# Eight offsets for the weight tiles and three pass sequences, in place of one of each

## The chip, the cores and the metric

The kernel runs on one core of a Trainium2 chip. The metric is the device time of one execution in microseconds (us). A profiled execution gives, beside its time, a trace of every instruction on every engine: TensorE (PE, with its weight loads as PEld), VectorE (DVE), ScalarE (ACT), GpSimd (POOL) and SyncE (SP).

## What is computed

Two decoder layers on 256 tokens of width 2048, in float32. The first mixes by retention, the second by sliding-window attention; after each comes a gated feed-forward with a short convolution:

```
for i in range(DEPTH):                       # DEPTH = 2
    hn = rmsnorm(h, norm_mix_g[i])
    h = h + (retention(hn, ...) if i == 0 else sliding_window_attention(hn, ...))
    hn = rmsnorm(h, norm_ffn_g[i])
    u = hn @ w_up                            # 2048 x 11008
    c = conv_b + sum(pad(u)[:, j:j+S] * conv_w[j] for j in range(3))
    a, b = split(c, 2)
    h = h + (silu(a) * b) @ w_down           # 5504 x 2048
return rmsnorm(h, final_norm_g)
```

Retention projects to q and k (8 heads of 256), v and a gate (8 heads of 512) and back; attention projects to 32 query heads and 4 key and value heads of 64 and back. Almost all of the work is in these projections.

## The kernel before

Every weight is read once from HBM, in transfers of up to 1 MB: a `Unit` is one transfer of up to 2048 columns per partition (several chunks of 128 weight rows side by side), and the units form one list over the whole kernel. Each number is split in two parts of reduced precision, hi and lo: ScalarE makes hi of a raw tile (L161), VectorE makes lo as the rest (L162), in pieces of 1024 columns, some way ahead of TensorE, into four buffers of each. Activations are split likewise into tiles xT, yT and zT, a chunk being [128, 2, 256]: 256 columns of hi and 256 of lo.

A product is then three parts: hi by hi, hi by lo, lo by hi. There are two forms. `products` (L256 to L258) holds a slice of the activations stationary and moves 512 (for the values of attention 256) weight columns past it, three passes into one PSUM bank. It makes v and the gate of retention, the values of attention and all projections back. `products_tr` gives a transposed result and is used for q, k and the up-projection. It holds 128 weight columns stationary and moves the activations: a long pass (L267) holds hi weights and moves 512 columns, activations hi and lo at once; a short pass (L269) holds lo weights and moves 256. A chunk of a group has two 128-column halves with a bank each. In the letters that the change uses, H and h are the long passes of the first and second half, L and l the short ones, and the sequence is HhLl.

hi and lo tiles are 2048 + 64 columns wide, so that a unit's data can be set off from the tile's start. The offset `at` is 48 columns (192 bytes) in each unit that has a transposed group, and 0 in all others. In the built program all buffers of hi, lo, xT, yT, zT, v, vs, sch and pT begin on a multiple of 256 bytes within a partition, and the slices that a pass takes are whole multiples of 256 bytes further on. So the distance between the stationary slice and the moving chunk, modulo 256 bytes, is 4 x `at` in `products_tr`, and 0 in `products`, but for the values of attention, which share a unit with the keys and so have 192 bytes on the moving side (that is 64, counted from the moving to the stationary slice). Transposes (L276) hold a slice of h, pr or y stationary and move the identity; the tile h lies 32 bytes past a multiple of 64 bytes, pr and y lie on one.

The order of work is set by Python as the program is written out: `run_main` walks over the units, emits a unit's passes, and calls `split_ahead` and a list of small tasks (evictions, norms, scores) between chunks. The scheduler leaves this order as it is.

Of the kernel before, what the change touches and what calls it, by code (L numbers as in the profile page):

```python
# [16 lines left out]
P = 128  # L17
D = 2048
S = 256
# [26 lines left out]
RAW = 2  # L46
SPLIT = 1024

ASIDE = 48
F_CUTS = [0, 14, 28, NF]  # L50
START = (1, 1, 2, 2, 2)

# [57 lines left out]
class Kernel:  # L110
# [37 lines left out]
    def splits(self, i):  # L148

        u = self.units[i]  # L150
        nc = self.nc
        w = u.n * u.cols
        at = ASIDE if any(g.tr for g in u.groups) else 0
        u.hi, u.lo = (
            self.wp.tile([P, 2048 + 64], F32R, tag=tag, name=tag, bufs=AHEAD + 1)[:, at : at + w]
            for tag in ("hi", "lo")
        )
        for c in range(0, w, SPLIT):
            e = min(c + SPLIT, w)
            raw, hi, lo = (x[:, c:e] for x in (u.raw, u.hi, u.lo))  # L160
            nc.scalar.copy(out=hi, in_=raw)  # L161
            nc.vector.tensor_tensor(out=lo, in0=raw, in1=hi.bitcast(F32), op=ALU.subtract)  # L162
            yield e / w
# [29 lines left out]
    def run_main(self):  # L193
        for i, u in enumerate(self.units):
            self.load_to(i + AHEAD + RAW)
            self.split_ahead(i)
            for g in u.groups:
                if g.ps is None:
                    if g.begin:
                        g.begin()  # L200
                    g.ps = self.banks(g)
            if u.groups[0].by_token:
                break
            for j, g in enumerate(u.groups):
                c0 = sum(x.cols for x in u.groups[:j])
                for kk, ch in enumerate(u.chunks):
                    sl = slice(kk * u.cols + c0, kk * u.cols + c0 + g.cols)
                    if g.tr:
                        self.products_tr(g, u.hi[:, sl], u.lo[:, sl], u.act[ch])
                    else:  # L210
                        for t in range(2):
                            out = g.ps[t] if g.apart else g.ps[:, t]
                            self.products(g, out, t, u.hi[:, sl], u.lo[:, sl], u.act[ch])
                    g.seen += 1
                    self.step += g.cols / 512
                    if g.seen == g.total:
                        g.done(g)
                    share = (self.step - u.at) / u.steps
                    self.split_ahead(i, share - 1e-6)
                    self.run_tasks()  # L220
        self.run_by_token(self.units[i:])
        while self.tasks:
            self.step += 1
            self.run_tasks()
# [32 lines left out]
        nc.tensor.matmul(out, lhsT=ah, rhs=lo, start=False, stop=False)  # L257
        nc.tensor.matmul(out, lhsT=al, rhs=hi, start=False, stop=last)  # L258

    def products_tr(self, g, hi, lo, act):  # L260

        nc = self.nc
        first, last = g.seen == 0, g.seen == g.total - 1
        both = act.rearrange("p x s -> p (x s)")
        tiles = [(g.ps[:, i], slice(i * P, (i + 1) * P)) for i in range(2)]
        for out, sl in tiles:
            nc.tensor.matmul(out, lhsT=hi[:, sl], rhs=both, start=first, stop=False)  # L267
        for out, sl in tiles:
            nc.tensor.matmul(  # L269
                out[:, :S], lhsT=lo[:, sl], rhs=act[:, 0], start=False, stop=last  # L270
            )


    def transposes(self, ps, ins):
# [683 lines left out]
```

## Time and profile before

| | |
|---|---|
| median of 2 runs | 2431.38 us (2431.19 to 2431.57) |
| the profiled execution's own time | 2431.45 us |
| its span, first to last instruction | 2429.3 us |
| mean granted TensorE clock | 0.999 |
| PE busy | 2413.0 us (99%), 12676 matmuls |
| DVE busy | 1554.9 us (64%) |
| ACT busy | 1224.6 us (50%) |
| moved by DMA | 460.27 MB, mean 189 GB/s |

The span is what the trace covers, 2 us less than the time of the execution. Matmuls are pipelined: a record's end is modelled, records overlap, and so the time that a pass takes on the engine is read from start to start.

### The profile page before, as it was taken

The numbers are of one execution on the slowest core, as the hardware profiler recorded it, in microseconds if no ns is written. First come the engines' busy times: TensorE is split into PE (matmuls) and PEld (weight loads), VectorE is DVE, ScalarE is ACT, GpSimd is POOL, SyncE is SP. The second block draws the span as 40 slices with busy tenths as digits, with TensorE's granted clock in tenths as the row PEclk, the third lists the DMA queues.
The fourth block names the chain that finished last, engine by engine and source line by source line (L and its number), as shares of the span: only waits on it lengthen the run. The fifth ranks groups of instructions, "written<-read, shape, count | busy, mean of one in ns | idle before, by whom it ended". The sixth has DMA issues, their size and how long they took to land.

```text
span 2429.3 us, 31370 instructions
## 1 busy us (share of the span) xinstructions
PE 2413.0 (99%) x12676; PEld 2060.6 (85%) x12676; DVE 1554.9 (64%) x2104; ACT 1224.6 (50%) x1782; POOL 29.2 (1%) x37
## 2 busy tenths in 40 slices
PE   8999999999999999999999999999999999999998
PEld 7888888888888888888888888888888888888887
DVE  6555555554556775677577756876777477657774
ACT  6444344344445553555355545765555355535553
POOL 3000000000000000000000000000000000000000
PEclk9999999999999999999999999999999999999999
DMA  8655555555554555555555555445454555554553
GB/s 287 213 187 180 192 181 186 185 188 182 182 191 168 199 185 194 192 192 183 197 192 195 194 182 195 182 156 193 174 194 174 207 191 191 190 207 175 195 200 126
DMA packets 68977, 460.27 MB, mean 189 GB/s; under 512 B 8032, under 2 KB 9184, under 8 KB 16736
## 3 DMA queue, kind: packets, MB, share of 16 engines
q1 hardware_dynamic: 68544, 457.23, 52.7%
q8 instruction: 99, 1.62, 0.3%
q10 hardware_dynamic: 288, 1.05, 0.1%
q14 instruction: 46, 0.38, 0.0%
HBM read 456.15 MB, written 2.10 MB: 189 GB/s over the span
## 4 chain that ended last, share of the span: by engine, by line
PE 97%; DMA 1%; issue 1%; POOL 0%; DVE 0%; ACT 0%; SPq 0%; POOLq 0%; DVEq 0%; ACTq 0%
PE mm L267 33%; PE mm L269 17%; PE mm L256 13%; PE mm L258 12%; PE mm L257 12%; PE po L256 2%; PE po L258 2%; PE po L257 2%; PE po L393 1%; PE ms L276 1%; PE ms L679 1%; PE ms L503 0%; POOL acc L309 0%; DMA h<-in_xT 0%; DVE lo L162 0%
## 5 line engine op out<-in xcount | busy, mean ns | idle before, releaser
L162 DVE TENSOR_TENSOR lo<-raw,hi 128x1024 fp32r<-128x1024 f32 (+1 forms) x849 | 1018.4, 1219 | 612.3 <-ACT hi L161 611.9
L161 ACT CAST hi<-raw 128x1024 fp32r<-128x1024 f32 (+1 forms) x849 | 857.8, 1042 | 522.5 <-PE mm L258 332.3
L267 PE MATMUL mm<-xT,hi 128*128 128x512 f32 x3552 | 1107.9, 393 | 6.2 <-DVE xT L323 6.2
L269 PEld LDWEIGHTS mm<-xT,lo 128*128 128x128 f32 x3552 | 667.3, 188 | 150.3 <-DVE lo L162 3.1
L269 PE MATMUL mm<-xT,lo 128*128 128x256 f32 x3552 | 702.2, 279 | 1.1 <-DVE lo L162 1.0
L267 PEld LDWEIGHTS mm<-xT,hi 128*128 128x128 f32 x3552 | 540.5, 188 | 11.7 <-ACT hi L161 6.2
L256 PE MATMUL mm<-hi,zT 128*128 128x512 f32 x688 | 268.3, 390 | 0.0
L258 PE MATMUL mm<-hi,zT 128*128 128x512 f32 x688 | 267.7, 389 | 0.0
L257 PE MATMUL mm<-lo,zT 128*128 128x512 f32 x688 | 267.7, 389 | 0.0
L601 DVE SCALAR_TENSOR_TENSOR cv<-u,cw,cv 128x255 f32<-128x255 f32 x344 | 158.3, 481 | 6.1
L256 PE MATMUL mm<-hi,yT 128*128 128x512 f32 x384 | 153.3, 399 | 0.0
L258 PEld LDWEIGHTS mm<-hi,zT 128*128 128x128 f32 x688 | 129.1, 188 | 27.0
L257 PEld LDWEIGHTS mm<-lo,zT 128*128 128x128 f32 x688 | 129.2, 188 | 26.5
L256 PEld LDWEIGHTS mm<-hi,zT 128*128 128x128 f32 x688 | 129.1, 188 | 26.4
L258 PE MATMUL mm<-hi,yT 128*128 128x512 f32 x384 | 149.8, 390 | 0.0
L257 PE MATMUL mm<-lo,yT 128*128 128x512 f32 x384 | 149.7, 390 | 0.0
L378 ACT COPY u<-mm 128x512 f32<-128x512 f32 x86 | 50.4, 586 | 183.7 <-PE mm L269 183.7
L379 DVE TENSOR_TENSOR u<-mm,u 128x512 f32<-128x512 f32 x86 | 59.5, 692 | 93.2 <-ACT u L378 93.2
L594 ACT ACTIVATE cv<-u,cw 128x256 f32<-128x256 f32 x172 | 94.2, 595 | 48.7 <-DVE u L388 48.7
L611 ACT CAST zT<-cv 128x256 fp32r<-128x256 f32 x86 | 34.9, 406 | 156.2 <-DVE cv L609 156.2
L256 PE MATMUL mm<-hi,xT 128*128 128x512 f32 (+1 forms) x288 | 109.1, 379 | 0.0
L258 PE MATMUL mm<-hi,xT 128*128 128x512 f32 (+1 forms) x288 | 108.6, 377 | 0.0
(118 smaller groups left out, 1784.1 us busy)
## 6 DMA issues: line engine op xcount, KB each, us to landing
raw<-in_up SPq DMA_DIRECT2D x172, 1024.0 KB, 4.7
raw<-in_ret_in SPq DMA_DIRECT2D x94, 1024.0 KB, 4.8
raw<-in_dn SPq DMA_DIRECT2D x72, 1024.0 KB, 4.8
raw<-in_ret_out SPq DMA_DIRECT2D x32, 1024.0 KB, 4.7
raw<-in_qkv SPq DMA_DIRECT2D x20, 1024.0 KB, 4.7
raw<-in_att_out SPq DMA_DIRECT2D x14, 1024.0 KB, 4.7
raw<-in_dn SPq DMA_DIRECT2D x16, 512.0 KB, 3.2
raw<-in_dn SPq DMA_DIRECT2D x8, 768.0 KB, 4.3
```

Of the source, the lines that this page charges most:

```text
L161: nc.scalar.copy(out=hi, in_=raw)
L162: nc.vector.tensor_tensor(out=lo, in0=raw, in1=hi.bitcast(F32), op=ALU.subtract)
L256: nc.tensor.matmul(out, lhsT=ah, rhs=hi, start=first, stop=False)
L257: nc.tensor.matmul(out, lhsT=ah, rhs=lo, start=False, stop=False)
L258: nc.tensor.matmul(out, lhsT=al, rhs=hi, start=False, stop=last)
L267: nc.tensor.matmul(out, lhsT=hi[:, sl], rhs=both, start=first, stop=False)
L269: nc.tensor.matmul(out[:, :S], lhsT=lo[:, sl], rhs=act[:, 0], start=False, stop=last)
L378: nc.scalar.copy(out=x, in_=g.ps[:, :, S:])
L379: nc.vector.tensor_tensor(out=x, in0=g.ps[:, :, :S], in1=x, op=ALU.add)
L594: nc.scalar.activation(out=c[:, half], in_=u[:, half], func=AF.Identity, scale=w[:, 2:3], bias=w[:, 3:4])
L601: nc.vector.scalar_tensor_tensor(out=c[:, half, d:], in0=u[:, half, : S - d], scalar=w[:, 2 - d : 3 - d], in1=c[:, half, d:], op0=ALU.mult ...
L611: nc.scalar.copy(out=z[:, 0], in_=s)
```

## The change

The one offset becomes a list of eight, taken in turn by a unit's number in the list of all units. A unit's number divided by eight, modulo three, gives its `order`: 0 keeps HhLl; 1 is HLhl; 2 is HhLl with every other chunk turned round to LlHh (not the last chunk of a group). Units without a transposed group keep offset 0 and use no order. Of 1776 transposed chunks, 672 become HLhl, 224 become LlHh and 880 stay HhLl. Of 3552 long passes (and as many short ones) 448 each have the offsets 0, 12, 16, 40 and 44, 432 have 48, 428 have 52 and 452 have 56.

```
-ASIDE = 48
+ASIDE = (56, 52, 48, 44, 40, 16, 12, 0)
...
-        at = ASIDE if any(g.tr for g in u.groups) else 0
+        at = ASIDE[i % len(ASIDE)] if any(g.tr for g in u.groups) else 0
+        u.order = i // len(ASIDE) % 3
...
-                        self.products_tr(g, u.hi[:, sl], u.lo[:, sl], u.act[ch])
+                        self.products_tr(g, u.hi[:, sl], u.lo[:, sl], u.act[ch], u.order)
...
-        tiles = [(g.ps[:, i], slice(i * P, (i + 1) * P)) for i in range(2)]
-        for out, sl in tiles:
-            nc.tensor.matmul(out, lhsT=hi[:, sl], rhs=both, start=first, stop=False)
-        for out, sl in tiles:
-            nc.tensor.matmul(
-                out[:, :S], lhsT=lo[:, sl], rhs=act[:, 0], start=False, stop=last
-            )
+        seq = {0: "HhLl", 1: "HLhl", 2: "HhLl"}[order]
+        if order == 2 and g.seen % 2 and not last:
+            seq = "LlHh"
+        for x in seq:
+            i = int(x.islower())
+            out, sl = g.ps[:, i], slice(i * P, (i + 1) * P)
+            if x in "Hh":
+                nc.tensor.matmul(out, lhsT=hi[:, sl], rhs=both, start=first, stop=False)
+            else:
+                nc.tensor.matmul(
+                    out[:, :S], lhsT=lo[:, sl], rhs=act[:, 0], start=False, stop=last
+                )
```

On TensorE, in the first two chunks of the q and k weights of the second retention head (a unit of offset 0 and order 1), the program of before has these rows. The names are out<-moving,stationary with buffer numbers; "x2" is two in a row. L267 is the long line, L269 the short one.

```order
L267 MATMUL mm_693<-xT_118,hi_594 128x512 x2
L269 MATMUL mm_693<-xT_118,lo_595 128x256 x2
L267 MATMUL mm_693<-xT_120,hi_594 128x512 x2
L269 MATMUL mm_693<-xT_120,lo_595 128x256 x2
L393 MATMUL po_708<-v_539,sch_569 128x512 x3
```

In the program after, where the long line is L275, the short one L277 and the attached products L401, the same place reads:

```order
L275 MATMUL mm_693<-xT_118,hi_594 128x512
L277 MATMUL mm_693<-xT_118,lo_595 128x256
L275 MATMUL mm_693<-xT_118,hi_594 128x512
L277 MATMUL mm_693<-xT_118,lo_595 128x256
L275 MATMUL mm_693<-xT_120,hi_594 128x512
L277 MATMUL mm_693<-xT_120,lo_595 128x256
L275 MATMUL mm_693<-xT_120,hi_594 128x512
L277 MATMUL mm_693<-xT_120,lo_595 128x256
L401 MATMUL po_708<-v_539,sch_569 128x512 x3
```

Long and short passes take turns; the work of other lines stands where it stood. One unit later (offset 56, order 2) TensorE had, before:

```order
L267 MATMUL mm_693<-xT_142,hi_632 128x512 x2
L269 MATMUL mm_693<-xT_142,lo_633 128x256 x2
L267 MATMUL mm_693<-xT_144,hi_632 128x512 x2
L269 MATMUL mm_693<-xT_144,lo_633 128x256 x2
L267 MATMUL mm_693<-xT_152,hi_632 128x512 x2
```

and after:

```order
L275 MATMUL mm_693<-xT_142,hi_632 128x512 x2
L277 MATMUL mm_693<-xT_142,lo_633 128x256 x2
L277 MATMUL mm_693<-xT_144,lo_633 128x256 x2
L275 MATMUL mm_693<-xT_144,hi_632 128x512 x2
L275 MATMUL mm_693<-xT_152,hi_632 128x512 x2
```

The four short passes of two chunks now stand together, and so do the four long ones around the next border. The order of instructions on ScalarE, SyncE and GpSimd is the same in both programs; VectorE's is too, with a few waits for TensorE left out.

## Rows read from the trace of the kernel before

**Rows 1.** The page: busy time of each engine, and the granted clock in 40 slices.
```profile
PE 2413.0 (99%) x12676; PEld 2060.6 (85%) x12676; DVE 1554.9 (64%) x2104; ACT 1224.6 (50%) x1782; POOL 29.2 (1%) x37
...
PEclk9999999999999999999999999999999999999999
```

**Rows 2.** The page: the chain that ended last, by line.
```profile
PE mm L267 33%; PE mm L269 17%; PE mm L256 13%; PE mm L258 12%; PE mm L257 12%; PE po L256 2%; PE po L258 2%; PE po L257 2%; PE po L393 1%; PE ms L276 1%; PE ms L679 1%; PE ms L503 0%; POOL acc L309 0%; DMA h<-in_xT 0%; DVE lo L162 0%
```

**Rows 3.** Waits of PE: who for whom, us in total, times, longest.
```profile
PE mm L267 <- DVE xT L323: 6.2, 1, 6.2
PE mm L269 <- DVE lo L162: 1.0, 3, 0.5
```

**Rows 4.** Timeline of PE at 790 us: start us, us, line, count.
```profile
790.28 0.62 PE L267 MATMUL mm<-xT,hi 128*128 128x512 f32 x2
790.74 0.39 PE L269 MATMUL mm<-xT,lo 128*128 128x256 f32 x2
790.97 0.62 PE L267 MATMUL mm<-xT,hi 128*128 128x512 f32 x2
```

**Rows 5.** PE groups by line and form: count, busy us, mean ns, idle before.
```profile
L267 PE MATMUL mm<-xT,hi 128*128 128x512 f32 x3552 | 1107.9, 393 | 6.2 <-DVE xT L323 6.2
L269 PE MATMUL mm<-xT,lo 128*128 128x256 f32 x3552 | 702.2, 279 | 1.1 <-DVE lo L162 1.0
L256 PE MATMUL mm<-hi,zT 128*128 128x512 f32 x688 | 268.3, 390 | 0.0
...
L257 PE MATMUL mm<-lo,zT 128*128 128x512 f32 x688 | 267.7, 389 | 0.0
...
L393 PE MATMUL po<-pT,vs 128*64 128x256 f32 x96 | 16.3, 278 | 0.0
...
L257 PE MATMUL mm<-lo,xT 128*128 128x256 f32 x32 | 9.0, 281 | 0.0
```

**Rows 6.** The same groups in five windows of some 50 ns from 1000.49 us.
```profile
L267 PE MATMUL mm<-xT,hi 128*128 128x512 f32 x1 | 0.4, 388 | 0.0
...
L267 PE MATMUL mm<-xT,hi 128*128 128x512 f32 x1 | 0.4, 392 | 0.0
L269 PE MATMUL mm<-xT,lo 128*128 128x256 f32 x1 | 0.3, 283 | 0.0
...
L269 PE MATMUL mm<-xT,lo 128*128 128x256 f32 x1 | 0.3, 280 | 0.0
...
L267 PE MATMUL mm<-xT,hi 128*128 128x512 f32 x1 | 0.4, 394 | 0.0
L269 PE MATMUL mm<-xT,lo 128*128 128x256 f32 x1 | 0.3, 276 | 0.0
```

**Rows 7.** Instructions of L267, L269 and L257: duration ns min/median/max.
```profile
L267 PE MATMUL mm<-xT,hi x3552: 387/392/794, 6.2 to 2338.6; 128*128 128x512 f32 x198
...
L269 PE MATMUL mm<-xT,lo x3552: 276/280/415, 7.3 to 2339.0; 128*128 128x256 f32 x198
...
L257 PE MATMUL mm<-lo,zT x688: 387/389/398, 905.7 to 2420.3; 128*128 128x512 f32 x172
```

**Rows 8.** Instructions of L276, the transposes: duration ns min/median/max.
```profile
L276 PE MATMUL ms<-ident,h x96: 270/272/273, 696.4 to 1716.9; 128*128 128x128 f32 x96
L276 PE MATMUL ms<-ident,pr x96: 272/272/273, 1514.0 to 1661.6; 128*128 128x128 f32 x96
```

**Rows 9.** Groups: the weight loads of L269, and the splits on DVE and ACT.
```profile
L269 PEld LDWEIGHTS mm<-xT,lo 128*128 128x128 f32 x3552 | 667.3, 188 | 150.3 <-DVE lo L162 3.1
...
L162 DVE TENSOR_TENSOR lo<-raw,hi 128x1024 fp32r<-128x1024 f32 (+1 forms) x849 | 1018.4, 1219 | 612.3 <-ACT hi L161 611.9
L161 ACT CAST hi<-raw 128x1024 fp32r<-128x1024 f32 (+1 forms) x849 | 857.8, 1042 | 522.5 <-PE mm L258 332.3
```

More of the change, by code (lines that the diff above doesn't have):

```diff
@@ L258, in products, with products_tr @@
         nc.tensor.matmul(out, lhsT=al, rhs=hi, start=False, stop=last)
-    def products_tr(self, g, hi, lo, act):
+    def products_tr(self, g, hi, lo, act, order):
         nc = self.nc
```

## Prediction

> **What bounds the kernel now.** The first view is the share of busy time, and it leaves one candidate: TensorE is busy 2413.0 of 2429.3 us, and its granted clock is at full speed in all 40 slices [rows 1], so there is no slow clock to win back. The chain of waits says the same from the other end: nearly all of it is TensorE's own matmuls, half of them the two lines that the change touches [rows 2]. TensorE's waits are the third view: one of 6.2 us for the first activations and three of 1.0 us in all for a lo tile, both where the kernel starts [rows 3]. So nothing that VectorE, ScalarE or a transfer does can be won on this path. What counts is the time from one matmul's start to the next one's start, times their number.
>
> That time has to be read with care, because a matmul's record is longer than its share of the engine. In the steady stretch at 790 us one chunk (two long, two short passes) repeats every 0.69 us [rows 4], while the four records of such a chunk, at the means, last 2 x 393 + 2 x 279 = 1344 ns [rows 5]. The record is longer than the step by (1344 - 690) / 4, about 163 ns, in every pass. So a pass whose record is 4 ns longer costs 4 ns, and differences of records are prices.
>
> **What the change does, part by part.** It moves nothing between engines. The same 3552 long and 3552 short passes run on the same tiles. Two things differ for them: how far the stationary slice lies from the moving chunk (modulo 256 bytes; the moving chunks all lie on multiples of 256 bytes), and which pass follows which.
>
> *Sequence.* The records of two chunks that follow each other, pass by pass [rows 6], are H 388, h 392, L 283, l 280 and then H 392, h 394, L 276, l 276 (the second H and l repeat figures of rows that stand there). Averaged over the two chunks, a long pass before a load of hi costs 390 and before a load of lo 393; a short pass before a load of lo costs 279.5, before a load of hi 278. I take the price of a pass to hang on its own length and on what is loaded under it. In HLhl both long passes stand before lo and both short ones before hi: 2 x 393 + 2 x 278 = 1342 against 390 + 393 + 279.5 + 278 = 1340.5, so +1.5 ns for each of 672 chunks, +1.0 us. In a pair HhLl LlHh, three of four long passes stand before hi and three of four short ones before lo: 3 x 390 + 393 + 3 x 279.5 + 278 = 2679.5 against 2681, so -1.5 ns for each of 224 pairs, -0.3 us. Sum +0.7 us. That H and L of HLhl add into the same bank one after the other needs no price: the other product lines do so three times in a row and have records of 390 and 389 [rows 5].
>
> *Distance.* Per group of offsets, each some 448 long and as many short passes:
> Offset 48 (192 bytes, 432 passes of each kind) is as before: 0.
> Offset 0 gives distance 0. The rows at that distance are the products with zT: 390 and 389, so 389.5 against 393, -3.5 ns. The short pass at distance 0 has a near row only with a half-wide stationary slice, 278 against 279, -1 ns [rows 5]. 448 x 4.5 = -2.0 us.
> Offset 16 gives 64 bytes. The short passes at 64 bytes are those of the values of attention: 281, +2 ns each [rows 5]. A long pass at 64 bytes doesn't stand in the trace; between 389 and 393, and I take 391, -2 ns. Sum 0.
> Offsets 12, 40, 44, 52 and 56 (48, 160, 176, 208, 224 bytes) have no row for these passes: 2224 long, 2224 short. The lower bound is that each falls to the shortest record seen, 387 rounded up to 388 and 276 [rows 6, 7]: 2224 x (5 + 3) = -17.8 us. The upper bound is that each rises to the longest unwaited one, 398 (products with lo) and 283: 2224 x (5 + 4) = +20.0 us [rows 6, 7]. What speaks for a small value: a transpose whose stationary slice starts 32 bytes past a multiple of 64 has the same record, 272, as one that starts on it [rows 8], so the start by itself isn't priced. I take the step that the two shown nonzero distances differ by, +2 ns, for the short passes and nothing for the long ones: 2224 x 2 = +4.4 us.
>
> The Trainium skill (TensorE: Matmul & The Clock Gate, "Step-by-step: what each phase is for") says that the moving operand and the weight load have read ports of their own, so that a load takes nothing from the running pass; by that rule the distance terms are all zero, which is the third rival below. The trace agrees in size, not to the nanosecond: median 392 at 192 bytes, 389 at 0.
>
> *What lies beside it.* ScalarE and VectorE write hi and lo at other offsets, 849 splits of 1042 and 1219 ns on engines that are 50% and 64% busy [rows 1, 9]. TensorE never waits for them after the start [rows 3], so a dearer write is hidden; without that cover each of the 444 splits of these transfers would put its increase on the path. HLhl wants lo one long pass (about 0.23 us) earlier at a transfer's start, LlHh frees hi two short passes (0.23 us) later; four buffers of each hide both. SyncE's and GpSimd's queues keep their order and pass nothing new.
>
> **Sum.** The profiled execution took 2431.45 us, 0.07 above the median of the runs, so I use it as it is: 2431.45 + 0.7 - 2.0 + 0 + 4.4 = 2434.5 us. A measurement of this kernel can tell about 2%, 48.6 us, from no change; this is far inside.
>
> **Rivals.**
> *Collisions at the unseen distances (slower).* If the stationary read and the moving read meet in the same part of a row, each pass loses time as long as the load runs. The largest step between two otherwise equal passes is 276 to 283, 7 ns [rows 6]. On all 4448 passes at unseen distances, in place of the +4.4: 2430.1 + 31.1 = 2461 us. It passes 2% at about 11 ns per pass. For it: records do differ by up to 7 ns at one and the same distance, so something is met or missed. Against: 0, 64 and 192 bytes lie within 4 ns of each other.
> *Short passes bound by the load (slower by over 2%).* A load's record lasts 188 ns [rows 9], more than a short pass's step of 115 ns (0.23 us for two) [rows 4]. If an uneven start keeps a load from overlapping, the short pass takes as long as the load: 73 ns x 2224 = 162 us, 2592 us. Against it: 188 ns fits under a step of 115 ns in all of the trace, and the step follows the columns.
> *Offsets are of no account (the change doesn't do what it says).* Each pass costs what it did, and the sequence term alone is left: 2432.2 us.
> *The stalls go (faster).* 192 bytes is a poor distance and the unseen ones are free: -17.8 in place of +4.4, 2412 us.
>
> **How the numbers follow.** My forecast gets 0.50 and the third rival 0.25, since rows at three distances lie so close. Collisions get 0.13, stalls that go 0.08, load-bound short passes 0.04. The range reaches from 2420 (a bit over half of the way to the faster rival) to 2454 (collisions of some 5 ns): with forecast and third rival, and about a third of those two rivals, 0.8 lies in it. Faster by over 2% would need 27 ns from every chunk of 1776, while the shortest records leave 16, so 0.01; slower by over 2% is the load-bound case and the tail of collisions, 0.05; within 2% 0.94.
>
> **What the profile after would show.** Right: mean records of the long and short lines within 2 ns of 393 and 279, grouped by transfer with no group over 2 ns from the rest, the same 6.2 and 1.0 us of waits, full clock. If transfers of one offset show a chunk of 0.72 us or more beside 0.69 in their neighbours, collisions are the cause. If transfers of HLhl do so at all offsets, my pricing of a pass by what is loaded under it is wrong. I would be wrong above all if a distance that isn't a multiple of 64 bytes is dear, for which the trace has no row on these lines.

## The result, and the profile after

The changed kernel takes 2445.67 us (2445.57 to 2445.77, two runs) against 2431.38 us: ratio 1.0058, 95% interval 1.0038 to 1.0078. It is slower by 14.3 us, or 0.6%, and the interval doesn't include 1. The forecast was 2434.5 us, slower by 3.1 us, with a range that holds the measured time.

At first sight the profile after looks like the one before. Its page has the busy time of each engine and the granted clock in 40 slices, to be laid beside [rows 1]:

```profile
PE 2427.4 (99%) x12676; PEld 2066.5 (85%) x12676; DVE 1554.6 (64%) x2104; ACT 1224.7 (50%) x1782; POOL 29.2 (1%) x37
...
PEclk9999999999999999999999999999999999999999
```

TensorE is busy 14.4 us longer, the span grew by 14.1 us (2429.3 to 2443.4), the other engines did what they did, and the clock is full throughout. The waits of TensorE answer to [rows 3]:

```profile
PE mm L275 <- DVE xT L331: 6.2, 1, 6.2
PE mm L277 <- DVE lo L164: 0.8, 2, 0.5
```

So no wait was added on the lines of the change. The time lies in the passes themselves, and the groups by line, which answer to [rows 5], say in which:

```profile
L275 PE MATMUL mm<-xT,hi 128*128 128x512 f32 x3552 | 1132.3, 395 | 6.2 <-DVE xT L331 6.2
L277 PE MATMUL mm<-xT,lo 128*128 128x256 f32 x3552 | 780.4, 280 | 0.9 <-DVE lo L164 0.8
L258 PE MATMUL mm<-hi,zT 128*128 128x512 f32 x688 | 268.3, 390 | 0.0
```

The long line went from 393 to 395 ns and the short one from 279 to 280; the products that the change leaves alone stayed at 390. Times 3552 that is some 11 us with whole nanoseconds, and 14 us when the steps from start to start are summed. (The busy sums of the two lines grew much more than that, since records that no longer stand in pairs overlap less; they can't be compared between sequences.)

Means hide what the timeline shows. These are rows of TensorE's timeline after (start us, duration us, line, count), the first and the eighth chunk of a transfer with offset 48 and of one with offset 40, both HhLl, a few microseconds apart:

```profile
835.97 0.63 PE L275 MATMUL mm<-xT,hi 128*128 128x512 f32 x2
...
840.82 0.62 PE L275 MATMUL mm<-xT,hi 128*128 128x512 f32 x2
...
847.08 0.63 PE L275 MATMUL mm<-xT,hi 128*128 128x512 f32 x2
...
852.03 0.63 PE L275 MATMUL mm<-xT,hi 128*128 128x512 f32 x2
```

Seven chunks take 4.85 us at offset 48, 693 ns each, and 4.95 us at 40, 707 ns each; before, a chunk took 690 [rows 4]. Two transfers with one other between them differ in rate by 2%, with the same instructions on the same engine.

### The profile page after: what moved, and what is told of

It reads as the page before. It is cut to its first block, busy times and chain, and to the rows that moved or that the text cites. A ratio compares the mean times of both kernels' runs of the same rounds, so it can differ in the third digit from the quotient of the medians.

```text
span 2443.4 us, 31370 instructions
## 1 busy us (share of the span) xinstructions
PE 2427.4 (99%) x12676; PEld 2066.5 (85%) x12676; DVE 1554.6 (64%) x2104; ACT 1224.7 (50%) x1782; POOL 29.2 (1%) x37
## 4 chain that ended last, share of the span: by engine, by line
PE 97%; DMA 1%; issue 1%; POOL 0%; ACT 0%; DVE 0%; SPq 0%; POOLq 0%; ACTq 0%
PE mm L275 33%; PE mm L277 17%; PE mm L258 12%; PE mm L260 12%; PE mm L259 12%; PE po L258 2%; PE po L260 2%; PE po L259 2%; PE po L401 1%; PE ms L284 1%; PE ms L687 1%; PE ms L511 0%; POOL acc L317 0%; DVE lo L164 0%; DMA h<-in_xT 0%
## 5 line engine op out<-in xcount | busy, mean ns | idle before, releaser
L275 PE MATMUL mm<-xT,hi 128*128 128x512 f32 x3552 | 1132.3, 395 | 6.2 <-DVE xT L331 6.2
L277 PE MATMUL mm<-xT,lo 128*128 128x256 f32 x3552 | 780.4, 280 | 0.9 <-DVE lo L164 0.8
L277 PEld LDWEIGHTS mm<-xT,lo 128*128 128x128 f32 x3552 | 636.8, 188 | 80.4 <-DVE lo L164 2.9
L275 PEld LDWEIGHTS mm<-xT,hi 128*128 128x128 f32 x3552 | 606.8, 188 | 86.8 <-ACT hi L163 6.2
L258 PE MATMUL mm<-hi,xT 128*128 128x512 f32 (+1 forms) x288 | 109.2, 379 | 0.0
L259 PE MATMUL mm<-lo,xT 128*128 128x512 f32 (+1 forms) x288 | 108.6, 377 | 0.0
```

Source lines behind the costliest of these rows:

```text
L258: nc.tensor.matmul(out, lhsT=ah, rhs=hi, start=first, stop=False)
L277: nc.tensor.matmul(out[:, :S], lhsT=lo[:, sl], rhs=act[:, 0], start=False, stop=last)
```

## The experiments

All are versions of the changed kernel; where nothing else is said, each compares with the kernel before on the same chip. "ns a chunk" is the mean step from a chunk's first pass to the next chunk's, taken from the starts in the trace, without chunks into which other work falls. In the kernel before it is 690.3.

**The sequences alone, and the offsets alone.** order_only sets `ASIDE = (48,) * 8` and keeps the three sequences; offsets_only keeps the eight offsets and sets `u.order = 0`.

```
-ASIDE = (56, 52, 48, 44, 40, 16, 12, 0)
+ASIDE = (48,) * 8                          # order_only
...
-        u.order = i // len(ASIDE) % 3
+        u.order = 0                        # offsets_only
```

Expected of order_only: 

> Offset 48 everywhere, the three sequences in turn as in the change. Own step for each pair of offset and sequence (read off the later chunks of each transfer in the trace of the change): HLhl at 48 takes 706 ns a chunk against 690, turned-round pairs 696; 672 x 16 + 448 x 6 ns = +13.5 us, 2445 us. Separate prices for sequence and distance, as in the prediction: +0.7 us, 2432 us. Cost only at borders between transfers of unlike offset: none here, 2431 to 2433 us.

Expected of offsets_only: 

> The eight offsets in turn, HhLl everywhere. Own step for each pair: HhLl steps of 694 to 707 ns at the seven other offsets give +12.5 us, 2444 us, so each half of the change alone costs nearly as much as both. Separate prices: what the change cost less 0.7 us, 2445 us; then order_only must stay at 2432. Border cost alone: also about 2445, but then the later chunks of each transfer are back at 690 ns.

Measured: order_only 2437.26 us against 2430.67, ratio 1.0026 (1.0016 to 1.0037), +6.6 us; offsets_only 2442.57 us, 1.0048 (1.0031 to 1.0065), +11.9 us. The groups of offsets_only, by line:

```profile
L275 PE MATMUL mm<-xT,hi 128*128 128x512 f32 x3552 | 1115.8, 395 | 6.3 <-DVE xT L331 6.3
L277 PE MATMUL mm<-xT,lo 128*128 128x256 f32 x3552 | 706.0, 280 | 0.4 <-DVE lo L164 0.3
```

Both halves cost. 6.6 + 11.9 is 18.5 us, and together they took 14.3; the three intervals (about 2.5, 4.1 and 4.9 us to either side) are too wide to call that a difference. Cost at borders alone falls with order_only, which has no border between unlike offsets, and with the later chunks of offsets_only: from the fifth of a transfer on, the mean is 691 at 48 and 693 to 707 at the seven others. A border is not free, though: at offset 16 the first four chunks took 703 and the later ones 694, so the steps of kernels that take offsets in turn hold some of what the transfer before left. For order_only the first theory was too high by 8 us. The steps in its own trace say why: HLhl at 48 ran at 698 ns in some transfers and at 706 in others, 699 in the mean, while the trace of the change had 698 in one of its transfers and about 706 in the others. A pair of offset and sequence does not always have one step.

**A step for each offset.** scan16 gives the units 16 offsets in turn (`ASIDE = tuple(range(0, 64, 4))`, `u.order = 0`).

> HhLl everywhere, all 16 offsets 0, 4, ... 60 in turn, to read a step for each from the trace. Own step for each pair: the eight known offsets repeat their steps (0: 697, 12: 693, 16: 693, 40: 707, 44: 700, 48: 690, 52: 700, 56: 693 ns), and the mean is some 697 ns, 2443 to 2446 us. If offsets are of no account and neighbours alone set the cost, the eight do not repeat. An offset under 690 ns would be a faster kernel.

Measured in one run: 2448.41 us. The ns a chunk at each offset, beside those of offsets_only:

```
offset         0    4    8   12   16   20   24   28   32   36   40   44   48   52   56   60
scan16       698  706  702  701  695  701  704  702  697  703  707  699  693  700  694  701
offsets_only 696            694  698                           707  697  692  700  695
```

Seven of the eight repeat within 3 ns, offset 12 does not (694 and 701). No offset beats 48, and no group of them is flat: the step goes up and down by 1 to 8 ns from each to the next. The four multiples of 64 bytes (offsets 0, 16, 32, 48) lie at 693 to 698, the twelve others at 694 to 707.

**Is it the distance?** all_shifted is the kernel before with every tile 64 bytes lower, weights and activations alike. uni40_HhLl has offset 40 for all transposed units (`ASIDE = (40,)`, `u.order = 0`). both_moved has that too, but moves the activations as well, until all distances are again those of the kernel before.

```
-        const.tile([P, 40], F32, name="free")
+        const.tile([P, 24], F32, name="free")              # all_shifted, ASIDE = (48,), order 0
...
+        at = 40 if any(g.tr for g in u.groups) else 56 if u.act is self.xT else 0
...
-            x = self.acts.tile([P, 2, S], F32R, tag="xT", name="xT", bufs=NC)
+            x = self.acts.tile([P, 2 * S + 64], F32R, tag="xT", name="xT", bufs=NC)
+            x = x[:, 56 : 56 + 2 * S].rearrange("p (x s) -> p x s", x=2)   # both_moved, order 0
```

Expected of all_shifted: 

> The kernel before with a spacer 64 bytes smaller, so that every tile (weights and activations alike) starts 64 bytes lower modulo 256; distances between stationary and moving slices are unchanged. If only the distance counts: 690 ns a chunk and 2431.4 us. If the place of the weight slice itself counts: another step, as other offsets have (693 to 707 ns), 2437 to 2461 us.

Expected of uni40_HhLl: 

> Offset 40 for every transposed unit, HhLl everywhere. The trace of the change shows 707 ns a chunk for this pair wherever it stands. A step that belongs to the offset: 1776 x 16.5 ns = +29 us, 2460 us. A cost that needs unlike neighbours: none here, 2431 us. The prediction's price (2 ns a short pass): +7 us, 2438 us.

Expected of both_moved: 

> HhLl everywhere, weights of transposed units at offset 40 as in uni40_HhLl, but the xT chunks moved 32 bytes down as well (and the other weights that run with xT moved along), so that every distance is again that of the kernel before. If the distance between stationary weights and moving chunk is what counts: 690 ns a chunk, 2431 us. If it is the weights' own place: 700 to 707 ns as in uni40_HhLl, 2452 us.

Measured: all_shifted 2430.89 us, ratio 1.0001 (0.9991 to 1.0010). uni40_HhLl 2452.47 us, 1.0088 (1.0071 to 1.0105), +21.2 us. both_moved 2431.25 us, 1.0002 (0.9993 to 1.0012). The groups of uni40_HhLl, by line:

```profile
L275 PE MATMUL mm<-xT,hi 128*128 128x512 f32 x3552 | 1122.1, 397 | 6.6 <-DVE xT L331 6.6
L277 PE MATMUL mm<-xT,lo 128*128 128x256 f32 x3552 | 704.3, 279 | 0.3 <-DVE lo L164 0.3
```

and the same groups of both_moved, whose weights lie at the same offset 40:

```profile
L275 PE MATMUL mm<-xT,hi 128*128 128x512 f32 x3552 | 1108.5, 393 | 6.2 <-DVE xT L332 6.2
L277 PE MATMUL mm<-xT,lo 128*128 128x256 f32 x3552 | 703.4, 279 | 0.9 <-DVE lo L164 0.9
```

The long passes go from 393 to 397 when the weights move by 32 bytes, and back to 393 when the activations follow. So it is the distance that costs, and not the weights' own place. Nor is it what ScalarE and VectorE make of an uneven place, since they write the weights to it in both kernels.

uni40_HhLl cost 21 us and not 29 because it too has two steps. In its timeline, chunks at 758 and at 1000 us (start us, duration us, line, count; L284 are transposes):

```profile
757.24 0.60 PE L284 MATMUL ms<-ident,h 128*128 128x128 f32 x4
757.60 0.71 PE L275 MATMUL mm<-xT,hi 128*128 128x512 f32 x2
...
758.38 0.63 PE L275 MATMUL mm<-xT,hi 128*128 128x512 f32 x2
...
759.09 0.63 PE L275 MATMUL mm<-xT,hi 128*128 128x512 f32 x2
...
1000.23 0.63 PE L275 MATMUL mm<-xT,hi 128*128 128x512 f32 x2
...
1000.93 0.63 PE L275 MATMUL mm<-xT,hi 128*128 128x512 f32 x2
```

After transposes and a long pair that took 0.08 us more, chunks step by 0.71 us; at 1000 us, with the same offset and sequence, by 0.70 (707 and 700 ns). Each pattern holds for dozens of chunks, from one disturbance to another. In this trace each of the 23 chunks that come right behind transposes and are some 0.08 us longer is followed by 707; that the delay is what switches the pattern was read off and not tested.

**Does HLhl cost by itself?** uni56_HLhl (`ASIDE = (56,)`, `u.order = 1`) and uni48_HLhl (`ASIDE = (48,)`, `u.order = 1`).

Expected of uni56_HLhl: 

> Offset 56, HLhl everywhere. A step that belongs to the pair of offset and sequence: 693.3 ns in place of 690, +6 us, 2437 us, below the 699 to 707 ns that HLhl takes at 48. A price of HLhl itself, whatever the offset (from 48: 9 to 16 ns a chunk): +16 to +28 us, 2447 to 2459 us.

Expected of uni48_HLhl: 

> Offset 48, HLhl everywhere: the prediction priced this pair at +1.5 ns a chunk, +2.7 us, 2434 us. In the traces it ran in two steady patterns, 698 and 706.7 ns a chunk: if the pattern that a transfer enters in is kept, the time is that of one of them or between, 2445 to 2460 us, well above uni56_HLhl with the same sequence (2436 us).

Measured: uni56_HLhl 2436.33 us, ratio 1.0021 (1.0011 to 1.0030), +5.1 us, at 693.7 ns a chunk. uni48_HLhl 2444.90 us, 1.0056 (1.0039 to 1.0073), +13.4 us, mostly in the pattern of 698. The long line of each, uni48_HLhl first:

```profile
L275 PE MATMUL mm<-xT,hi 128*128 128x512 f32 x3552 | 1250.1, 395 | 6.8 <-DVE xT L331 6.8
```

```profile
L275 PE MATMUL mm<-xT,hi 128*128 128x512 f32 x3552 | 1241.5, 392 | 6.2 <-DVE xT L331 6.2
```

With HLhl, 56 is the better offset by 8.6 us; with HhLl, 48 is (692 against 695 in offsets_only). So the sequence has no price apart from the distance.

**Can a chunk be priced pass by pass?** Both versions keep HhLl (`ASIDE = (48,)`, `u.order = 0`). hi48_lo40 puts hi at 48 and lo at 40 in all transposed units; scan_lo gives lo the 16 offsets in turn (`4 * (i % 16)` in place of 40).

```
+        lo_at = 40 if at else 0
         u.hi, u.lo = (
-            self.wp.tile([P, 2048 + 64], F32R, tag=tag, name=tag, bufs=AHEAD + 1)[:, at : at + w]
-            for tag in ("hi", "lo")
+            self.wp.tile([P, 2048 + 64], F32R, tag=tag, name=tag, bufs=AHEAD + 1)[:, o : o + w]
+            for tag, o in (("hi", at), ("lo", lo_at))
         )
```

Expected of hi48_lo40: 

> HhLl everywhere, hi tiles at offset 48, lo tiles at 40. At 40 the last short pass l, which holds lo while hi is loaded for the next, takes 125 ns against 115.5 at 48. If a pass pays for the slice that it holds itself: l stays at 125, L at 117, the long ones at 227.5 and 230.5, some 700 ns a chunk, 2449 us. If it pays for the slice loaded under it: l goes back to 115.5, while h and L pay for lo: 232 and 117, some 692 ns, 2435 us.

Expected of scan_lo: 

> HhLl everywhere, hi tiles at 48, lo tiles at 0, 4, ... 60 in turn. If hi and lo count by themselves, the spread over lo offsets is about half of that with both moved (690 to 707 ns), and the mean is some 694 ns, 2440 us. If only both together set the step, the spread is as wide as before. A lo offset under 690 ns would be a faster kernel.

Measured: hi48_lo40 2458.41 us, ratio 1.0112 (1.0092 to 1.0133), +27.1 us, 707 ns a chunk. Neither account holds: with hi at the good offset and lo at the bad one it is dearer than with both at the bad one (+21.2 us). Its steps are 232, 239, 118 and 117 ns; the pass h, at 230.5 before, took most of it, and H rose by 4 ns though its own slice and the one loaded under it lie where they did. Its groups by line:

```profile
L276 PE MATMUL mm<-xT,hi 128*128 128x512 f32 x3552 | 1129.0, 400 | 6.4 <-DVE xT L332 6.4
L278 PE MATMUL mm<-xT,lo 128*128 128x256 f32 x3552 | 706.5, 280 | 0.0
```

scan_lo took 2448.03 us in one run, with 692 ns at lo 48 and 693 to 708 elsewhere (693 at 36, 694 at 4, 708 at 56): as wide a spread as with both moved. The step belongs to the four passes and their distances together, and not to one pass by itself.

**How fine is it?** scan_fine has offsets 40 to 55, one column (4 bytes) apart, HhLl.

> HhLl everywhere, offsets 40, 41, ... 55 in turn. If the step depends on the distance in units of 16 bytes, four neighbours share a step and 48 to 51 stay at 690 ns. If each 4 bytes count, 47 and 49 differ from 48 by several ns; one under 690 ns would be a faster kernel. In the mean some 697 ns, 2444 us.

Measured in one run: 2451.26 us. The ns a chunk:

```
offset     40   41   42   43   44   45   46   47   48   49   50   51   52   53   54   55
scan_fine 707  697  703  707  698  699  700  700  694  700  700  718  700  698  700  705
```

Four bytes matter: 51 takes 18 ns more than 50 or 52. Rows of its timeline at offset 48 and, three transfers on, at 51 (two chunk starts each):

```profile
784.57 0.62 PE L275 MATMUL mm<-xT,hi 128*128 128x512 f32 x2
...
785.95 0.62 PE L275 MATMUL mm<-xT,hi 128*128 128x512 f32 x2
...
801.38 0.65 PE L275 MATMUL mm<-xT,hi 128*128 128x512 f32 x2
...
803.52 0.65 PE L275 MATMUL mm<-xT,hi 128*128 128x512 f32 x2
```

Two chunks take 1.38 us at 48, and three take 2.14 us at 51: 690 and 713 ns.

**Is it a matter of the transposed form?** scan_products leaves the transposed units as before and gives all others 16 offsets in turn (`at = ASIDE[0] if any(g.tr for g in u.groups) else 4 * (i % 16)`, with `ASIDE = (48,)`).

> Transposed units as before (48, HhLl); the other units, whose weights move past stationary activations (4752 passes of 512 columns at 226.7 ns), get offsets 0, 4, ... 60 in turn. If the distance counts in this form too, steps spread by several ns a pass and the time rises, at 3 ns on average by 14 us, to 2445 us; an offset under 226.7 ns would be a faster kernel. If only the mix of long and short passes makes distance count, nothing changes: 2431 us.

Measured in one run: 2454.62 us, some 23 us over the runs of before. The groups of the products with zT, which answer to the rows of L256 and L257 with zT in [rows 5]:

```profile
L258 PE MATMUL mm<-hi,zT 128*128 128x512 f32 x688 | 271.4, 394 | 0.0
L259 PE MATMUL mm<-lo,zT 128*128 128x512 f32 x688 | 271.3, 394 | 0.0
L260 PE MATMUL mm<-hi,zT 128*128 128x512 f32 x688 | 270.9, 394 | 0.0
```

394 against 390 and 389: the distance counts here too, with no short passes about. Mean steps per pass ran from 228.4 ns at offset 0 and 228.5 at 60 to 234.6 at 52. Offset 0, which the kernel before has, is the best of them.

No version beat the kernel before.

## Why the prediction was right, and which of its terms were off

**What bounds the kernel** held: TensorE, at full clock, without new waits. What the prediction named as cover (the splits, the buffers, the queues) did cover: TensorE's waits stayed at 6.2 and 0.8 us.

**The direction** held: other distances make passes dearer, and both_moved shows that the distance is the cause (the same offset, 21 us dearer or not, by where the activations lie). In part that was luck. The sum is positive by one guessed term, 2 ns for each short pass at an unseen distance and nothing for the long ones; in offsets_only it was the long line that rose by 2 (393 to 395) and the short one by 1.

**Records as prices.** The prediction took a record that is 4 ns longer for 4 ns of cost. That held roughly. In uni40_HhLl the whole-nanosecond means grew by 4 for a long pass and 0 for a short one, 8 ns a chunk, and 21.2 us over 1776 chunks are 12.

**The term of distance** was mis-sized. The sum had -2.0 (offset 0), 0 (offset 16) and +4.4 us (the unseen ones), +2.4 in all; offsets_only measured +11.9. From its steps, borders included: offset 0 cost 696.1 - 690.3 = 5.8 ns on 224 chunks, +1.3 us; offset 16, 8.0 ns, +1.8 us; the unseen 12, 40, 44, 52 and 56 cost 3.8, 16.7, 6.4, 9.4 and 4.9 ns, together +9.1 us. The step that failed is the borrowing of prices from near rows: the products at distance 0 (389.5) and the values of attention at 64 bytes have another mix of passes, and a pass does not carry its price from one mix into another (hi48_lo40). Offset 0, the best for the products, is in the middle for HhLl. The bounds of the unseen distances, -17.8 and +20.0 us, held; the value inside them was half of what was needed.

**The term of sequence** was mis-sized too: +0.7 us, against +6.6 measured by order_only. Its ground, that a pass costs by its length and by what is loaded under it, is refuted by hi48_lo40, where H rose by 4 ns with its own slice and the one loaded under it in place. That sequence and distance have separate prices that add is refuted by uni48_HLhl (+13.4 us, priced at +2.7) and uni56_HLhl (+5.1): one sequence, two prices.

**The rivals.** Collisions, priced at 31 us and at 7 ns on each unseen pass, had the right sign and went too far: the dearest offset of the change, 40, took 17 ns more in a chunk of four passes, and only 51, in scan_fine, took 28, the full price. Offsets of no account falls: distance alone moved a chunk from 690 to 718 ns. The Trainium skill (TensorE: Matmul & The Clock Gate, "Step-by-step: what each phase is for") states separate read ports for the two operands, so that a load takes nothing from the running pass; the trace disagrees with that on these lines, though no run shows where the two operands meet. Load-bound short passes didn't occur: they would step by 188 ns, and their mean steps stayed between 114 and 125 ns at all offsets. Nor did the stalls go: no offset had a mean step below 690.

**The signs.** Line means of 395 and 280 lie within 2 ns of 393 and 279, which the prediction counted as right, while its other sign, no group of transfers off by more than 2 ns a pass, failed: 707 ns a chunk at offset 40 is 4 ns a pass. Means over a line hid it. Its chief worry, distances that aren't multiples of 64 bytes, came true in part: the dearest are all of that kind, but so are cheap ones (694 at 56).

**What stays open.** Why some distances are dear was not settled. Shown is that the step depends on the place of the stationary operand relative to the moving one, down to 4 bytes, and that chunks settle into a repeating pattern of steps, of which one setting can have two (700 and 707; 698 and 706). What makes a stretch fall into one or the other was not tested. Nothing in these traces tells what the two operands contend for; the loads of the two lines keep mean records of 188 to 189 ns in every run.

## What to carry to other kernels

When TensorE is busy all the time and its passes take some per cent more than their columns, move one operand by a few dozen bytes and measure: here the distance between the slice held and the chunk moved was worth up to 27 us of 2431, and nothing in waits or busy shares points to it. Look for it by giving each transfer another offset and reading steps by transfer, but confirm the winner in a uniform kernel, since neighbours and disturbances leave their mark on the pattern (offset 40 took 707 ns in turn with others and 702 on its own). A price per pass that was read in one sequence of passes didn't hold in another.

## What the runs showed of the hardware that was not expected

- At one granted clock (0.999) and with the same instructions, four passes of 1536 columns took 690 to 718 ns by the distance between stationary slice and moving chunk; 4 bytes changed it by up to 18 ns (offset 50 to 51).
- Steady steps of whole kernels fell on few values: 690, 693 to 694, 698, 700, 707 ns, alternating inside in repeats of one to three chunks (HhLl at 48 before: 687 and 693 in turn).
- The same instructions at the same offset had two steady rates, 700 and 707 ns a chunk, which held for tens of microseconds (uni40_HhLl).
